# Ten dot products of the modulation weights moved from the attention stage to the context steps, and the masks loaded earlier

## The chip, the core and the metric

The kernel runs on one core of a Trainium2 chip. The metric is the device time of one execution in microseconds (us). Before the change it is 1158.29 us, the median of three runs (1157.56 to 1158.67). The engines are named as in the profile: PE is TensorE (matmul), DVE is VectorE, ACT is ScalarE, POOL is GpSimd, SP is SyncE, which here only issues DMAs.

## The reference, cut to what matters

The program is one layer of a diffusion transformer: a gated linear attention (GLA) and a short convolution side by side, an output projection, then a convolutional feed-forward net. Six vectors of 1024 numbers modulate it, and they come from one small product:

```python
def adaln(cond, w, b):
    return jax.nn.silu(cond) @ w + b          # w: 1024 x 6144

sh1, sc1, gt1, sh2, sc2, gt2 = jnp.split(adaln(c, w_ada[i], b_ada[i])[:, None, :], 6, axis=-1)
hc = modulate(rmsnorm(ctx, g_pre_mix[i]), csh1, csc1)      # context: 256 tokens
kc, vc, gfc, gbc = gla_inputs(hc @ w_in[i][:, :COL_Q], *gla_p)
hx = modulate(rmsnorm(x, g_pre_mix[i]), sh1, sc1)          # 1024 tokens
yx = token_mixers(hx @ w_in[i], s_f, s_b, ...)             # needs the gates of every token
x = x + gt1 * rmsnorm(yx @ w_out[i], g_post_mix[i])
x = x + gt2 * rmsnorm(conv_ffn(modulate(...sh2, sc2)...), g_post_ffn[i])
```

The first two vectors (`sh1`, `sc1`) are needed at the start; `gt1`, `sh2`, `sc2` and `gt2` are needed only once the attention is done.

## The kernel before

All products run on PE in three passes of float32 split into a high and a low part (`mm3`, L142; the split is ACT for the high part, then a subtraction, L135). PE's order is the program's order in the whole kernel.

**The modulation weights.** Their product is no matmul: 48 blocks of 128 rows by 1024 (512 KB each) are loaded (L223), and DVE multiplies each with the broadcast condition and sums it (`ada_dot`, L230; 16 of the blocks twice, 64 dots). `some_ada(n)` (L555) first emits the dots of the loads that are pending and then issues n more loads. A load goes into a buffer of the pool `px` (tag x, eight buffers) or into the one buffer `ada` of `pgt`, in the rotation px, pgt, px. Four of the eight hold the split context `hch` and `hcl`, and two hold `kc` and `vc`, so that in the stage of this change two and one are left: three loads can be under way, and a load waits until the dot that read its buffer before has ended.

**The token-major stage (L568 to L617).** It forms keys, values and low-rank gate inputs with tokens on the partitions: eight steps `token_major(2, tk)`, two context steps for keys (L599 to L603), two context steps `token_major(2, NT + j)`, then the same ten steps for the other half of the values, `token_major(1, ...)`. The weights of that last group are split in two parts: `wa_split(1, kt)` for kt 0 to 3 is done at the last step tk = 7, for kt 4 to 7 at L609, just ahead of `token_major(1, 0)`. ACT, DVE and POOL follow the program's order here too. `put_aT` copies the gate inputs.

**The attention stage (L734 on).** A generator `gla` and a generator `stream` (the other input projections, as half blocks of 12 matmuls) are interleaved on PE. The first two steps have DVE in the program's order; after them a scheduler orders ACT, DVE, POOL and SP by its own estimate. Each of ten 128-token tiles (two of context, then c = 0 to 7) has one gate product (L484) into one of two banks of PSUM, three passes of ACT (absolute value, exponential, logarithm), and one DVE instruction (L493) that reads the bank and writes the log decay: `gc` for context, `g` for the others. A bank is free for the gate product after the next one only when L493 has read it. `sums` (L755) are the cumulative sums, `kx_prep` and `kx_turn` (L773 to L784) the scaled keys and their transposes. Between them stood ten more dots, each with its load in the one buffer of `pgt`:

```python
                some_ada(1, (pgt, "ada", 1))        # L830 and L839
                if c == 0:
                    V.tensor_copy(masks, mraw)      # L835
```

The masks are loaded at L625, behind the last load of the token-major stage. SP issues all DMAs in one order and waits for each one's buffer there; on eight lanes a DMA also waits for the one eight places before it.

Of the kernel before, what the change touches and what calls it, by code (L numbers as in the profile page):

```python
# [8 lines left out]
F32 = mybir.dt.float32  # L9
# [12 lines left out]
P = 128  # L22
# [4 lines left out]
DK = 64  # L27
# [92 lines left out]
def build(nc, ap, out, dbg=None):  # L120
    V, S, G, PE, SY = nc.vector, nc.scalar, nc.gpsimd, nc.tensor, nc.sync
    names = iter(range(10**9))

    def nm(s="t"):
        return f"{s}{next(names)}"

    def act(o, i, fn=AF.Copy, **kw):
        return S.activation(o, i, fn, **kw)  # L128
# [13 lines left out]
    def mm3(ps, lhs, rhs, first, last, more=False):  # L142

        (lh, ll), (rh, rl) = lhs, rhs
        PE.matmul(ps, lh, rh, start=first, stop=False, skip_group_check=more)  # L145
        PE.matmul(ps, lh, rl, start=False, stop=False, skip_group_check=more)  # L146
        PE.matmul(ps, ll, rh, start=False, stop=last, skip_group_check=more)  # L147

    with tile.TileContext(nc) as tc, tc.manual_schedule(engines={mybir.EngineType.PE}):  # L149
        pools = {}  # L150

        def popen(name, side=None, **kw):
            cm = tc.tile_pool(name=name, side=side, **kw)
            pools[name] = (cm, cm.__enter__())
            return pools[name][1]
# [19 lines left out]
        def bank(n):  # L175
            return pools[n][1].tile([P, 512], F32, tag=n, name=nm("ps"))
# [30 lines left out]
        px = popen("px", "right", bufs=8)  # L207
        pgt = popen("pgt", "left", bufs=1)
# [12 lines left out]
        def ada_load(j, pool, tag, bufs):  # L221
            raw = pool.tile([P, D], F32, tag=tag, bufs=bufs, name=nm("ada"))
            SY.dma_start(raw, ap["ada"][j])  # L223
            return raw

        def ada_dot(j, which, raw, eng=None):

            dst = (gcol, gctx)[which][:, j : j + 1]
            if eng is None:
                V.tensor_tensor_reduce(raw, raw, cbs[which], 1.0, 0.0, ALU.mult, ALU.add, dst)  # L230
            else:
                eng.tensor_tensor(raw, raw, cbs[which], ALU.mult)
                act(raw, raw, AF.Copy, accum_out=dst)
# [4 lines left out]
        def ada_affine_ctx(ft):  # L238

            V.tensor_tensor(am[:, 0, ft : ft + 4, 1], gctx[:, ft : ft + 4], col("bada", ft, 4), ALU.add)  # L240
            V.tensor_tensor(am[:, 1, ft : ft + 4, 1], gctx[:, 8 + ft : 12 + ft], bsc1[:, ft : ft + 4], ALU.add)
            V.tensor_tensor(am[:, 1, ft : ft + 4, 1], am[:, 1, ft : ft + 4, 1], col("g1", ft, 4), ALU.mult)
# [47 lines left out]
        def wa_load(g, kt):  # L290
            lo = (None, 256, 528)[g]
            wars[g, kt] = pst.tile([P, 272], F32, tag="waraw", bufs=6, name=nm("war"))
            SY.dma_start(wars[g, kt], ap["wa"][kt][:, lo : lo + 272])
# [203 lines left out]
        def ctx_load():  # L497
            for j in range(NCT):
                cxs.append(x_load(ap["ctx"], j))
                cdg.append(rms_diag(cxs[j]))  # L500
# [22 lines left out]
        def hc(kt, j):  # L523
            s = slice(j * P, (j + 1) * P)
            return hch[kt // 4][:, kt % 4, s], hcl[kt // 4][:, kt % 4, s]

        def token_major(g, tk, lhs, vv):
            pp = bank(ps_mm)
            for kt in range(KT):
                mm3(pp[:, :272], lhs(kt), (wah[g, kt], wal[g, kt]), kt == 0, kt == KT - 1)  # L530
            if g == 1:
                act(vv[:, :272], pp[:, :272])
                return
            al = cp.tile([P, 32], F32, tag="al", bufs=3, name=nm("al"))
            act(al, pp[:, 240:272])
            act(vv[:, 272:], pp[:, :240])
            als[tk] = al

        def put_aT(tk):
            pt = bank(ps_ms)  # L540
            PE.transpose(pt[:32, :P], als[tk], ident)
            s = slice(tk * P, (tk + 1) * P)
            act(aT[0:32, s], pt[:32, :P])
            V.tensor_tensor(aT[32:64, s], pt[:32, :P], aT[0:32, s].bitcast(F32), ALU.subtract)
            V.tensor_copy(aT[64:96, s], pt[:32, :P])

        def xlhs(tk):
            s = slice(tk * P, (tk + 1) * P)
            return lambda kt: (hxh[kt][:, s], hxl[kt][:, s])
# [5 lines left out]
        def some_ada(n, where=None):  # L555

            for a, raw in pend:
                ada_dot(a[0], a[1], raw, a[2])
            pend.clear()
            for _ in range(n):  # L560
                a = next(adas, None)
                if a is not None:
                    where_ = where or ((px, "x", 8), (pgt, "ada", 1), (px, "x", 8))[nada[0] % 3]
                    pend.append((a, ada_load(a[0], *where_)))
                    nada[0] += 1

        als = {}
        with tc.manual_schedule(engines={mybir.EngineType.Activation, mybir.EngineType.DVE, mybir.EngineType.Pool}):  # L568
            ctx_load()
            some_ada(4)  # L570
            for hf in range(2):
                pq1 = bank(ps_mm)
                tsl = slice(hf * 512, hf * 512 + 512)
                for kt in range(KT):
                    mm3(pq1, wq1[kt], (hxh[kt][:, tsl], hxl[kt][:, tsl]), kt == 0, kt == KT - 1)
                act(qh[hf][:, 1, :], pq1, AF.Copy, scale=DK ** -0.5)
            for t in range(NT):
                vt[t] = pvo.tile([P, VW], F32, tag="vo", name=nm("v"))
            for tk in range(NT):
                some_ada(3 if tk < 3 else 2 if tk < 5 else 1)  # L580
                if tk == 3:
                    ada_affine_ctx(0)
                if tk == 5:
                    ada_affine_ctx(4)
                if 4 <= tk < 8:
                    ctx_lo()
                token_major(2, tk, xlhs(tk), vt[tk])
                if tk > 1:
                    put_aT(tk - 2)
                if 3 <= tk < 7:  # L590
                    ctx_lo = ctx_norm(tk - 3)
                if tk == NT - 1:
                    for kt in range(4):
                        wa_load(1, kt)
                        wa_split(1, kt)
            put_aT(NT - 2)
            kc = px.tile([P, NCT, QK], F32, tag="x", name="kc")
            vc = px.tile([P, NCT, VW], F32, tag="x", name="vc")
            for j in range(NCT):  # L599
                pp = bank(ps_mm)  # L600
                for kt in range(KT):
                    mm3(pp[:, :QK], hc(kt, j), (wah[0, kt][:, :QK], wal[0, kt][:, :QK]), kt == 0, kt == KT - 1)
                act(kc[:, j, :], pp[:, :QK])  # L603
            put_aT(NT - 1)
            for kt in range(4, KT):
                wa_load(1, kt)
            for j in range(NCT):
                token_major(2, NT + j, lambda kt: hc(kt, j), vc[:, j, :])
            for kt in range(4, KT):  # L609
                wa_split(1, kt)  # L610
            for tk in range(NT):
                some_ada(3 if tk < 2 else 2)
                token_major(1, tk, xlhs(tk), vt[tk])
                if 0 < tk <= NCT:
                    put_aT(NT + tk - 1)
            for j in range(NCT):
                token_major(1, NT + j, lambda kt: hc(kt, j), vc[:, j, :])  # L617
        pclose("pst")
# [2 lines left out]
        pg_ = popen("pg", "right", bufs=1)  # L621
        tc.keep_in_program_order(S.preload_act_table_set("natural_log_exp_and_others"))
        masks = pg_.tile([P, 6, DK], U8, name="masks")
        mraw = px.tile([P, 6, DK], F32, tag="x", name="mraw")
        SY.dma_start(mraw, ap["masks"])  # L625
        og_d = [dr.tile([4, P, H, P], F32, name=f"ogd{c}") for c in range(2)]
        sc_d = [dr.tile([4, P, H, P], F32, name=f"scd{c}") for c in range(2)]
        x1_d = [dr.tile([P, D], F32, name=f"x1d{c}") for c in range(NT)]
# [106 lines left out]
        def gla():  # L735
# [91 lines left out]
            slot = lambda c: su[c // 2][:, c % 2, :]  # L827
            for j in range(NCT):
                ctx_decay(j)
                some_ada(1, (pgt, "ada", 1))  # L830
                yield 1
            for c in range(NT):
                decay(c)
                if c == 0:
                    V.tensor_copy(masks, mraw)  # L835
                if 0 < c <= NCT:
                    ctx_keys(c - 1)
                if c > 1:
                    sums(c - 2)  # L839
                some_ada(1, (pgt, "ada", 1))  # L840
                if c == 4:
                    su = [px.tile([P, 2, 512], F32, tag="x", name=f"su{i}") for i in range(4)]
                    ctx_state()
                if c >= NT - 2:
                    kx_prep(0, c - NT + 2)
                yield 0.8 if c > 1 else 1
            some_ada(0)
            sums(NT - 2)
            yield 0.8
            sums(NT - 1)  # L850
# [818 lines left out]
```

## Time and profile before

| | |
|---|---|
| median of three runs | 1158.29 us |
| the profiled execution, its own time | 1158.03 us |
| its span (first to last instruction) | 1156.1 us |
| PE busy | 1120.6 us, 97% of the span |
| DVE busy | 871.7 us, 75% |
| ACT and POOL busy | 525.4 us and 493.2 us |
| mean granted clock of PE | 0.993 of full speed |
| DMA | 176.00 MB, mean 152 GB/s |
| loads of modulation weights | 64 of 512 KB, median 4.4 us from issue to landing |

An engine's busy time is the sum of its instructions. A timeline row gives the start, the time, the engine, the line and the operation, how many instructions are merged, and in brackets the idle time of the engine ahead of it with what ended it. A row of windows gives the busy time of each engine in a stretch, then the clock that PE was granted (1.00 is 2.4 GHz, 0.50 is 1.2 GHz), the share of time that the DMA engines were busy, and the rate.

### The profile page before, as it was taken

Reading aid. Unit: us, or ns where it says so; the run is one execution under the profiler, and the core shown is the slowest. Engines: PE = TensorE matmul, PEld = TensorE weight load, DVE = VectorE, ACT = ScalarE, POOL = GpSimd, SP = SyncE. Lnnn points to the kernel's source line nnn. Section 1 sums busy time; section 2 is a strip of 40 time slices with the busy share of each in tenths; the row PEclk is TensorE's granted clock in tenths of the full one; section 3 lists DMA queues with packets and bytes.
Section 4 is the critical chain, followed back from the end, with each engine's and each line's share of the span. In section 5 each row is a group of like instructions: output and inputs, shape, how many; then the busy total and the mean of one; then the engine's idle time right before and its main releaser. Section 6 shows DMA issues by size and latency. Waiting matters only on the chain. (4 is left out here: it accounts for less than half of the span.)

```text
span 1156.1 us, 16906 instructions
## 1 busy us (share of the span) xinstructions
PE 1120.6 (97%) x6272; PEld 927.1 (80%) x6272; DVE 871.7 (75%) x1195; ACT 525.4 (45%) x943; POOL 493.2 (43%) x467
## 2 busy tenths in 40 slices
PE   7899988999999999999999999999999999999997
PEld 6689977888887878887887788888888888888885
DVE  4976647899778456576888978787878787778576
ACT  5745156644343456556233343333333345544443
POOL 3211012247457111128777868687768780000002
PEclk9999999999999999999999999999999999999999
DMA  9883853421113273232343323232323169978572
GB/s 345 281 305 137 268 142 125 149 63 47 56 44 90 67 272 114 91 110 73 91 146 108 105 98 118 92 110 92 118 85 116 65 213 343 346 236 286 196 245 100
DMA packets 80132, 176.00 MB, mean 152 GB/s; under 512 B 9807, under 2 KB 21711, under 8 KB 80050
## 3 DMA queue, kind: packets, MB, share of 16 engines
q1 hardware_dynamic: 80050, 174.93, 45.6%
q8 instruction: 49, 0.80, 0.3%
q14 instruction: 33, 0.27, 0.1%
HBM read 142.12 MB, written 32.78 MB: 151 GB/s over the span
## 5 line engine op out<-in xcount | busy, mean ns | idle before, releaser
L1341 DVE SCALAR_TENSOR_TENSOR y<-u,cols,y 128x945 f32<-128x945 f32 (+2 forms) x176 | 214.6, 1221 | 3.7 <-ACT y L128 1.3
L145 PE MATMUL ps<-mx,p 128*128 128x512 f32 x440 | 173.6, 395 | 3.3 <-DVE g L1396 2.2
L146 PE MATMUL ps<-mx,p 128*128 128x512 f32 x440 | 172.9, 393 | 0.0
L147 PE MATMUL ps<-mx,p 128*128 128x512 f32 x440 | 172.7, 393 | 0.0
L135 POOL TENSOR_TENSOR p<-rs,p 128x512 fp32r<-128x512 f32 x88 | 115.3, 1315 | 86.5 <-ACT p L128 82.7
L641 POOL TENSOR_TENSOR wl<-wr,wh 128x256 fp32r<-128x256 f32 x64 | 61.2, 985 | 160.8 <-ACT wh L128 160.7
L147 PE MATMUL ps<-p,p 128*128 128x512 f32 x308 | 120.1, 390 | 0.2
L146 PE MATMUL ps<-p,p 128*128 128x512 f32 x308 | 119.9, 389 | 0.0
L145 PE MATMUL ps<-p,p 128*128 128x512 f32 x308 | 119.8, 389 | 0.0
L145 PE MATMUL ps<-hxh,wh 128*128 128x512 f32 x256 | 104.6, 408 | 1.0 <-DVE sc L699 1.0
L230 DVE CUSTOM_DVE_ANT_0 ada<-ada,cb 128x1024 f32<-128x1024 f32 x64 | 80.2, 1269 | 31.4 <-DMA ada<-in_ada 31.0
L145 PEld LDWEIGHTS ps<-mx,p 128*128 128x128 f32 x440 | 82.6, 188 | 26.2 <-ACT u L128 5.4
L147 PE MATMUL ps<-hxh,wl 128*128 128x512 f32 x256 | 100.8, 394 | 0.0
L146 PE MATMUL ps<-hxl,wh 128*128 128x512 f32 x256 | 100.6, 393 | 0.0
L128 ACT ACTIVATE p<-rs 128x512 fp32r<-128x512 f32 x88 | 54.5, 622 | 100.4 <-POOL rs L1191 100.4
L147 PEld LDWEIGHTS ps<-mx,p 128*128 128x128 f32 x440 | 82.6, 188 | 18.6
L146 PEld LDWEIGHTS ps<-mx,p 128*128 128x128 f32 x440 | 82.6, 188 | 18.3
L135 POOL TENSOR_TENSOR p<-wr,p 128x512 fp32r<-128x512 f32 x58 | 76.1, 1312 | 13.1 <-ACT p L128 13.1
L128 ACT ACTIVATE y<-u,cols 128x1024 f32<-128x1024 f32 x22 | 26.6, 1209 | 105.1 <-DVE u L1403 105.1
L145 PE MATMUL ps<-b,p 128*128 128x512 f32 x176 | 69.7, 396 | 0.0
L147 PE MATMUL ps<-b,p 128*128 128x512 f32 x176 | 69.5, 395 | 0.0
L146 PE MATMUL ps<-b,p 128*128 128x512 f32 x176 | 69.4, 395 | 0.0
(274 smaller groups left out, 2592.7 us busy)
## 6 DMA issues: line engine op xcount, KB each, us to landing
ada<-in_ada SPq DMA_DIRECT2D x64, 512.0 KB, 4.4
wr<-in_wu SPq DMA_DIRECT2D x48, 512.0 KB, 4.0
h<-hd SPq DMA_DIRECT2D x77, 256.0 KB, 4.6
hd<-h SPq DMA_DIRECT2D x73, 256.0 KB, 2.1
wdr<-in_wd SPq DMA_DIRECT2D x55, 256.0 KB, 4.1
wdr<-in_wd SPq DMA_DIRECT2D x22, 512.0 KB, 6.7
x<-in_x SPq DMA_DIRECT2D x16, 512.0 KB, 4.0
wr<-in_wb SPq DMA_DIRECT2D x16, 512.0 KB, 3.7
```

The lines of the kernel that those rows point to most:

```text
L128: return S.activation(o, i, fn, **kw)
L135: (eng or V).tensor_tensor(lo, raw, hi.bitcast(F32), ALU.subtract)
L145: PE.matmul(ps, lh, rh, start=first, stop=False, skip_group_check=more)
L146: PE.matmul(ps, lh, rl, start=False, stop=False, skip_group_check=more)
L147: PE.matmul(ps, ll, rh, start=False, stop=last, skip_group_check=more)
L230: V.tensor_tensor_reduce(raw, raw, cbs[which], 1.0, 0.0, ALU.mult, ALU.add, dst)
L641: eng.tensor_tensor(lo[:, k : k + 2], raw[:, k : k + 2], hi[:, k : k + 2].bitcast(F32), ALU.subtract)
L1341: V.scalar_tensor_tensor(y3[:, ro, co], u3[:, ri, ci], col("wcf", 9 * p + 3 * (dr_ + 1) + dc + 1), y3[:, ro, co], ALU.mult, ALU.add)
```

## The change

Two calls of `some_ada` are added at the context steps of the token-major stage (two loads each at two steps, three each at two more, ten in all), a third that only emits the last dots, ahead of the last two steps; the load of the masks moves there. The calls in `gla` go, and the cast of the masks moves from tile 0 to tile 1. Lines behind L617 move by three.

```diff
             for j in range(NCT):
                 pp = bank(ps_mm)
+                some_ada(2)
                 for kt in range(KT):
...
             for j in range(NCT):
+                some_ada(3)
                 token_major(2, NT + j, lambda kt: hc(kt, j), vc[:, j, :])
...
+            mraw = px.tile([P, 6, DK], F32, tag="x", name="mraw")
+            SY.dma_start(mraw, ap["masks"])
+            some_ada(0)
             for j in range(NCT):
                 token_major(1, NT + j, lambda kt: hc(kt, j), vc[:, j, :])
...
-        mraw = px.tile([P, 6, DK], F32, tag="x", name="mraw")
-        SY.dma_start(mraw, ap["masks"])
...
                 ctx_decay(j)
-                some_ada(1, (pgt, "ada", 1))
...
-                if c == 0:
+                if c == 1:
                     V.tensor_copy(masks, mraw)
...
-                some_ada(1, (pgt, "ada", 1))
...
-            some_ada(0)
```

DVE of the kernel before, from the last copies of the gate inputs of the token-major steps to the dots of the last group; `wal` is the low part of the weights of `token_major(1, ...)`, kt 4 to 7, and `ada` a block of modulation weights:

```order
L544 TENSOR_TENSOR aT<-ps_1258,aT 32x128
L545 CAST aT<-ps_1258 32x128
L135 TENSOR_TENSOR wal_1328<-war_1263,wah_1327 128x272
L135 TENSOR_TENSOR wal_1332<-war_1265,wah_1331 128x272
L135 TENSOR_TENSOR wal_1336<-war_1267,wah_1335 128x272
L135 TENSOR_TENSOR wal_1340<-war_1269,wah_1339 128x272
L230 ISA ada_1139,gcol<-ada_1139,cb_106 128x1024
```

The same place of DVE in the changed kernel (the numbers of the buffers differ):

```order
L230 ISA ada_1139,gcol<-ada_1139,cb_106 128x1024
...
L230 ISA ada_1208,gcol<-ada_1208,cb_106 128x1024
...
L230 ISA ada_1210,gcol<-ada_1210,cb_106 128x1024
...
L230 ISA ada_1240,gcol<-ada_1240,cb_106 128x1024
...
L230 ISA ada_1242,gcol<-ada_1242,cb_106 128x1024
...
L230 ISA ada_1284,gcol<-ada_1284,cb_106 128x1024
...
L230 ISA ada_1286,gcol<-ada_1286,cb_106 128x1024
L230 ISA gcol 128x1
L230 ISA ada_1288,gcol<-ada_1288,cb_106 128x1024
L230 ISA gcol 128x1
L135 TENSOR_TENSOR wal_1356<-war_1274,wah_1355 128x272
```

Eight dots now stand ahead of the four splits, where none stood.

DVE of the kernel before at the first gates of the attention stage; the first `gc` frees the bank of the third gate product:

```order
L230 ISA ada_1554,gcol<-ada_1554,cb_106 128x1024
L230 ISA gcol 128x1
L835 CAST masks<-mraw 128x384
L493 SCALAR_TENSOR_TENSOR gc<-ps_1727,ge_1729 128x512
L230 ISA ada_1584,gcol<-ada_1584,cb_106 128x1024
L230 ISA gcol 128x1
L230 ISA ada_1586,gcol<-ada_1586,cb_106 128x1024
L230 ISA gcol 128x1
L493 SCALAR_TENSOR_TENSOR gc<-ps_1753,ge_1755 128x512
```

The same place in the changed kernel:

```order
L230 ISA ada_1584,gcol<-ada_1584,cb_106 128x1024
L230 ISA gcol 128x1
L230 ISA ada_1614,gcol<-ada_1614,cb_106 128x1024
L230 ISA gcol 128x1
L493 SCALAR_TENSOR_TENSOR gc<-ps_1759,ge_1761 128x512
L230 ISA ada_1616,gcol<-ada_1616,cb_106 128x1024
L230 ISA gcol 128x1
L837 CAST masks<-mraw 128x384
L1032 TENSOR_TENSOR gv_4206<-gcol,cols 128x8
L1033 TENSOR_TENSOR gv_4206<-gv_4206,cols 128x8
L493 SCALAR_TENSOR_TENSOR gc<-ps_1781,ge_1783 128x512
```

The first `gc` stood behind the masks and the third last dot of the token-major stage; it now stands behind the last dot but one of all.

DVE of the kernel before between the log decays of tile 6 and tile 7 (`sc` is the short convolution, `kx` the scaled keys):

```order
L493 SCALAR_TENSOR_TENSOR g_1969<-ps_1970,ge_1972 128x512
L773 TENSOR_TENSOR kx_1989<-bc_1720 128x1024
L689 TENSOR_TENSOR sc_1820<-sc_1820,ps_1955 128x512
L773 TENSOR_TENSOR kx_2030<-bc_1721 128x1024
L230 ISA ada_1864,gcol<-ada_1864,cb_106 128x1024
L230 ISA gcol 128x1
L776 TENSOR_TENSOR kx_1989<-kx_1989,kh_92 128x1024
L693 SCALAR_TENSOR_TENSOR sc_2006<-sc_1820,cols,sc_2006 128x8x63
L493 SCALAR_TENSOR_TENSOR g_1969<-ps_2011,ge_2013 128x512
L694 SCALAR_TENSOR_TENSOR sc_2006<-sc_1820,cols,sc_2006 128x8x63
```

And in the changed kernel:

```order
L493 SCALAR_TENSOR_TENSOR g_1976<-ps_1977,ge_1979 128x512
L776 TENSOR_TENSOR kx_1993<-bc_1752 128x1024
L692 TENSOR_TENSOR sc_1839<-sc_1839,ps_1962 128x512
L776 TENSOR_TENSOR kx_2031<-bc_1753 128x1024
L779 TENSOR_TENSOR kx_1993<-kx_1993,kh_92 128x1024
L696 SCALAR_TENSOR_TENSOR sc_2010<-sc_1839,cols,sc_2010 128x8x63
L697 SCALAR_TENSOR_TENSOR sc_2010<-sc_1839,cols,sc_2010 128x8x63
L493 SCALAR_TENSOR_TENSOR g_1976<-ps_2015,ge_2017 128x512
```

The dot between them is gone, and the second half of the convolution (L694, now L697) has moved ahead of the log decay of tile 7.

## Rows read from the trace of the kernel before

**Rows 1.** The page: the busy time of each engine over the span, and the rate of the DMAs in 40 equal slices of the span.

```profile
PE 1120.6 (97%) x6272; PEld 927.1 (80%) x6272; DVE 871.7 (75%) x1195; ACT 525.4 (45%) x943; POOL 493.2 (43%) x467
...
GB/s 345 281 305 137 268 142 125 149 63 47 56 44 90 67 272 114 91 110 73 91 146 108 105 98 118 92 110 92 118 85 116 65 213 343 346 236 286 196 245 100
```

**Rows 2.** Windows of 5 us in the attention stage: the stretch, then the busy time of PE, PEld, DVE, ACT and POOL with the number of instructions, the granted clock, the DMA share and GB/s.

```profile
155.00:160.00 5.00, 2.37 (x11) 1.64 (x10) 2.90 (x5) 2.43 (x5) 0.00 (x0) 1.00 0.26 39
...
170.00:175.00 5.00, 4.33 (x16) 3.84 (x17) 3.17 (x8) 3.02 (x8) 1.54 (x2) 0.66 0.68 197
...
200.00:205.00 5.00, 5.00 (x19) 4.38 (x19) 2.97 (x4) 2.05 (x8) 0.00 (x0) 0.51 0.45 177
```

**Rows 3.** Timeline of PE in the attention stage: gate products (L484), cumulative sums (L755), and the last matmul of a half block (194.91).

```profile
155.09 0.39 PE L484 MATMUL ps<-wgh,aT 98*128 98x512 f32 x1
158.12 0.50 PE L484 MATMUL ps<-wgh,aT 98*128 98x512 f32 x1 [2.63 <-DVE gc L493]
...
167.61 1.05 PE L755 MATMUL ps<-tri,g 128*128 128x128 f32 x8
170.67 0.76 PE L484 MATMUL ps<-wgh,aT 98*128 98x512 f32 x1 [2.01 <-DVE g L493]
...
191.42 1.13 PE L755 MATMUL ps<-tri,g 128*128 128x128 f32 x8 [0.34 <-DVE g L493]
...
194.91 0.39 PE L147 MATMUL ps<-hxh,wl 128*128 128x512 f32 x1
199.35 2.05 PE L755 MATMUL ps<-tri,g 128*128 128x128 f32 x8 [4.05 <-DVE g L493]
```

**Rows 4.** Timeline of DVE in the attention stage, with the idle time ahead of an instruction in brackets.

```profile
157.10 0.36 DVE L835 CAST masks<-mraw 128x384 uint8<-128x384 f32 x1 [3.18 <-DMA mraw<-in_masks]
157.38 0.68 DVE L493 SCALAR_TENSOR_TENSOR gc<-ps,ge 128x512 f32<-128x512 f32 x1
...
168.55 1.45 DVE L230 CUSTOM_DVE_ANT_0 ada<-ada,cb 128x1024 f32<-128x1024 f32 x1 [6.31 <-DMA ada<-in_ada]
...
169.94 0.68 DVE L493 SCALAR_TENSOR_TENSOR g<-ps,ge 128x512 f32<-128x512 f32 x1
...
183.75 1.22 DVE L230 CUSTOM_DVE_ANT_0 ada<-ada,cb 128x1024 f32<-128x1024 f32 x1 [2.38 <-DMA ada<-in_ada]
...
184.90 0.68 DVE L689 TENSOR_TENSOR sc<-sc,ps 128x512 f32<-128x512 f32 x1
...
194.05 1.76 DVE L230 CUSTOM_DVE_ANT_0 ada<-ada,cb 128x1024 f32<-128x1024 f32 x1
...
195.74 1.73 DVE L776 TENSOR_TENSOR kx<-kx,kh 128x1024 f32<-128x1024 f32 x1
...
198.52 0.68 DVE L493 SCALAR_TENSOR_TENSOR g<-ps,ge 128x512 f32<-128x512 f32 x1
199.12 0.73 DVE L694 SCALAR_TENSOR_TENSOR sc<-sc,cols,sc 128x504 f32<-128x504 f32 x1
199.78 1.21 DVE L776 TENSOR_TENSOR kx<-kx,kh 128x1024 f32<-128x1024 f32 x1
```

**Rows 5.** Timeline of ACT: the scaling of the short convolution that holds up ACT's queue ahead of the log decays of tiles 5 to 7.

```profile
185.62 0.82 ACT L128 ACTIVATE sc<-sc,cols 128x512 f32<-128x512 f32 x1 [1.92 <-DVE sc L689]
```

**Rows 6.** Timeline of SP in the token-major stage: the DMAs that it issued, merged (a row spans from the first issue to the last).

```profile
108.69 0.80 SPq L293 DMA_DIRECT2D war<-in_wa  x2
115.49 3.12 SPq L634 DMA_DIRECT2D wr<-in_wb  x2
118.70 33.01 SPq L223 DMA_DIRECT2D ada<-in_ada  x18
```

**Rows 7.** The tile of the modulation weights over the whole kernel: its dots on DVE (ns shortest, median, longest) and the time of its loads from issue to landing.

```profile
L230 DVE CUSTOM_DVE_ANT_0 ada<-ada,cb x64: 1208/1224/2323, 13.9 to 218.9; 128x1024 f32<-128x1024 f32 x64
...
DMA to landing us min/median/max: 3.5/4.4/9.0
```

**Rows 8.** Timeline of DVE in the token-major stage: the copies of the gate inputs (L545), the splits of the weights of kt 4 to 7 (L135), and dots.

```profile
110.04 0.28 DVE L545 CAST aT<-ps 32x128 fp32r<-32x128 f32 x1
...
113.80 0.28 DVE L545 CAST aT<-ps 32x128 fp32r<-32x128 f32 x1
119.90 1.50 DVE L135 TENSOR_TENSOR wal<-war,wah 128x272 fp32r<-128x272 f32 x4 [5.81 <-ACT wah L128]
121.31 1.22 DVE L230 CUSTOM_DVE_ANT_0 ada<-ada,cb 128x1024 f32<-128x1024 f32 x1
...
123.36 1.23 DVE L230 CUSTOM_DVE_ANT_0 ada<-ada,cb 128x1024 f32<-128x1024 f32 x1 [0.82 <-DMA ada<-in_ada]
...
131.35 1.22 DVE L230 CUSTOM_DVE_ANT_0 ada<-ada,cb 128x1024 f32<-128x1024 f32 x1
...
132.50 1.22 DVE L230 CUSTOM_DVE_ANT_0 ada<-ada,cb 128x1024 f32<-128x1024 f32 x1
...
152.69 1.22 DVE L230 CUSTOM_DVE_ANT_0 ada<-ada,cb 128x1024 f32<-128x1024 f32 x1 [1.33 <-DMA ada<-in_ada]
```

**Rows 9.** Windows of the dots alone: the stretch, DVE's busy time with the number of dots, the granted clock, the DMA share and GB/s.

```profile
140.00:155.00 15.00, 8.38 (x7) 1.00 0.85 279
```

**Rows 10.** Timeline of PE at the first step of the last group of the token-major stage: its first matmul, and the first that reads a low part of kt 4.

```profile
118.89 0.29 PE L145 MATMUL ps<-wah,hxh 128*128 128x272 f32 x1
...
120.52 0.29 PE L146 MATMUL ps<-wal,hxh 128*128 128x272 f32 x1
```

## The prediction, made before the changed kernel ran

> **What bounds the kernel now.** I read the page first: PE is busy for 1120.6 of 1156.1 us [rows 1], so only PE's own waits and PE's slow clock can be won. Listing PE's waits by stage, I find 9 of the 35 us of idle time in one stretch, 155 to 205 us, the start of the attention stage: 2.63 us ahead of the third gate product (158.12), 2.01 ahead of the sixth (170.67), 0.34 and 4.05 ahead of the last cumulative sums (191.42, 199.35), each ended by a log decay on DVE [rows 3]. The windows add that PE was granted 0.66 of full speed in 170 to 175 and 0.51 in 200 to 205, each time behind such a wait [rows 2]; that is 0.34 x 4.33 = 1.5 us and 0.49 x 5 = 2.45 us lost.
>
> DVE's timeline tells why the decays are late. The first stood behind the cast of the masks, which waited 3.18 us for its DMA; the one at 169.94 behind a dot that waited 6.31 us for its weights; between the decays of tiles 6 and 7 DVE did a dot from 194.05 to 195.74 [rows 4]. The change removes the masks from that place, and all ten dots. The question is what the ten cost where they go.
>
> **The token-major stage: DMAs.** Here DVE and the DMAs have room before, and PE runs without a gap. But the loads are a closed loop: three buffers, a median of 4.4 us from issue to landing, then a dot of 1.22 us [rows 7] that steps on by 1.15 (131.35 to 132.50), and only then the next issue. The 16 dots from 123.36 to 152.69 [rows 8] give 29.33 / 15 = 1.955 us each; (4.4 + 1.15) / 3 = 1.85 would be the loop with nothing else in it. So ten more loads cost about 19.6 us of loop time. Before, SP issued only small loads and two blocks of other weights between 108.69 and 118.70, and then 18 loads in 33.01 us [rows 6]; the new loads can fill those 10 us and not the rest.
>
> I step through it. The dot of the load that was already there follows the copies of the gate inputs (110.04 + 0.28, rows 8): 110.34. Behind it stand two dots whose buffers come free early, and SP has nothing else to issue until 108.69 [rows 6], so their loads have landed: 111.5 and 112.65, to 113.8, then a copy to 114.4. The dot at 110.34 frees a buffer at 111.6; its load lands 4.0 later (I take 3.5 to 4.4, few loads being under way), so the next dots stand at 115.6 and 116.75, then 117.9 (loaded 112.8 to 117). The buffer freed at 116.8 lands at 120.9: dots at 120.95 and 122.1, to 123.25.
>
> **A new wait at 120.5.** Only behind these eight dots come the four splits of kt 4 to 7. Before, they ran at 119.90 [rows 8], and PE read the first low part at 120.52 [rows 10], with no slack to speak of. Now the first split ends at 123.25 + 0.4 = 123.7: PE waits 3.2 us (2.5 to 4.5 by the same landing times). Nothing but the rest of this product is queued behind it on PE; ACT's evictions follow PE.
>
> **A longer wait at the third gate.** Behind the splits (1.5 us) the loop goes on: the dot after them at 124.7, the next, loaded at 122.2, at about 126.6. From that dot to the last but one, behind which the first log decay now stands, are 18 steps: 126.6 + 18 x 1.955 = 161.8, the decay at 163.0. PE follows a decay by 158.12 - 157.38 = 0.74 [rows 3, 4]: the third gate product comes at 163.7 in place of 158.12. That is 5.6 us late, and it swallows the wait at 120.5, since PE would arrive at 155.48 + 3.2 = 158.7. The step is 1.85 at the low end (1.9 us earlier) and 2.14 at the high end, as in 140 to 155, where seven dots took 15 us [rows 9] (3.3 us later); I take 1.955, the mean of the same loop.
>
> PE then sits idle for 5 us. The nearest wait, 4.05 us, was followed by 0.51 [rows 2], the shorter 2.63 by full speed. I count one such stretch, 2.45 us, less the 0.34 us or so that PE waits for the next gate's bank anyway: 2.1 us. Its ends are 0 and 2.45.
>
> A rule of the Trainium skill would give another end: DMA: Bandwidth & Descriptors, section Bandwidth, puts the limit of HBM to SBUF near 358 GB/s per core; as an estimate from it, 512 KB would take 1.46 us, and a loop bound by that would be faster than I have it. The trace does not agree in this stage, with 279 GB/s at a DMA share of 0.85 [rows 9]; by that rule the 18 steps end 9 us earlier.
>
> **What goes away in the attention stage.** Removed there: ten loads and ten dots of 1.2 us, which lay beside PE's work except where a decay stood behind them.
> - The decay at 169.94 had its bank's data long before; without the dot ahead of it, it runs by 165 and PE comes to 170.67 without the 2.01 us; the slow clock behind it (1.5 us) goes too. Both ends: 0 if that clock stays, 3.5; I take 3.5, since DVE has nothing else to do there.
> - The 0.34 us at 191.42: I take it as gone.
> - Tile 7. ACT's queue waited 1.92 us at 185.62 for the convolution on DVE [rows 5], which stood behind a dot that waited for its load (183.75, then 184.90); DVE had idled 2.38 us ahead of that dot, and would have taken the convolution then. So ACT is some 2 us earlier from there, and with it the decay of tile 6. Between the two decays DVE saves the dot (195.74 - 194.05 = 1.7) and gains the half convolution that is now ahead (199.78 - 199.12 = 0.66) [rows 4]. The decay of tile 7: 198.52 - 2 - 1.7 + 0.66 = 195.5, and 0.7 more for it. PE arrives at 194.91 + 0.39 = 195.3 [rows 3], and waits 0.9 in place of 4.05: 3.1 us. With so short a wait the slow clock of 200 to 205 goes too, 2.45. The ends are 0, if ACT's queue holds as before, and 6.5 with no wait left.
>
> The masks' cast costs 0.36 us behind the last dot; nothing at that place reads them. The two blocks of stream weights that SP issued from 115.49 on now stand behind loads; they are read only in the attention stage, past 155. The small write of the second row of gains moves ahead of two such blocks, for which nothing waits yet: 0, and at the other end a landing, 4.4 us, if one of them were late. From 205 us on PE works at 97% and more, so what is won or lost by then reaches the end.
>
> **The sum**, against the profiled execution's own 1158.03 us (span 1156.1 and 1.9 around it, 0.26 below the median of the runs): + 5.6 (third gate) + 2.1 (clock behind it) - 3.5 (170.67) - 0.3 - 3.1 - 2.5 (tile 7, wait and clock) = 1156.3 us.
>
> **The rivals.**
> 1. *The loads run at the rate of the DMA engines.* The first slice of the page moves 345 GB/s [rows 1]; 0.524 MB at that rate is 1.52 us, and 18 steps end at 126.6 + 27.4 = 154.0, before PE arrives at 158.7. Only the wait at 120.5 is left (158.7 in place of 158.12): + 0.6 in place of + 7.7, so 1149.2. For it: the added loads come at a quiet place. Against it: the loop of before never went so fast, with the same three buffers. 10%. The limit that the Trainium skill gives (DMA: Bandwidth & Descriptors, section Bandwidth) would fall on this side.
> 2. *Slower: ACT's order keeps tile 7 where it is.* ACT works through its queue in order, and its exponential of the scaled keys waits for DVE, the scaling for the convolution, and only then comes tile 7's absolute value. If that chain starts with PE's gate rather than with the dots, the 4.05 us and the slow clock behind them stay, 5.6 us, while the late third gate is paid: 1161.9. It decides from the point where tile 7's decay comes more than some 2.5 us behind PE's 195.3 on the old scale. For it: the decay of tile 6 waited for ACT, not for a dot. Against it: rows 5 show ACT itself waiting for DVE. A loop step of 2.14 adds 3.3 us and brings the same sign: 1159.6. 23% together.
> 3. *No change:* the late gate and the freed stage cancel to within 1 us, since PE only waits at another place: 1158. For it: both sums are near 8 and 9 us. 17%.
> 4. *My forecast*, 1156.3, 50%, with an own range of 1153.5 to 1159 from the ends of the loop step and the clock.
>
> **How the numbers follow.** A change of less than 0.2% (2.3 us) can't be told from none here; against the median that is 1156.0 to 1160.6. My forecast lies at this edge: 24 of its 50% below, 26 inside. Faster: 24 + 10 + 6 of rival 3 = 40%. Slower: 21 of rival 2's 23. Same: 26, 11 of rival 3 and 2 of rival 2, 39%. The range leaves out most of rival 1 and the top of rival 2: 1151.5 to 1161.8.
>
> **What would show it.** In the profile of the changed kernel: a wait of PE of about 3 us near 120.5 for a split (L135); a wait of about 5 us ahead of the third gate product for the first decay, DVE's dots going on to about 163 us in steps of 1.95, with waits for DMAs between; a slow clock behind it; no wait ahead of the sixth gate; under 1.5 us ahead of the last sums, at full clock. I would be wrong if the third gate comes within 2 us of its old time, or if tile 7's wait keeps its 4 us.

## The result, and the profile after

The changed kernel takes 1161.88 us (median of 22 runs, 1158.58 to 1166.58) against 1159.24 of the kernel before on the same chip (22 runs, 1157.27 to 1163.24): ratio 1.002, 95% interval 1.0011 to 1.0029. It is slower by 0.2%, where I had forecast 0.2% faster. The profiled execution has a span of 1159.4 us, 3.3 more than before.

PE's busy time on the page hardly moves [rows 1]; its waits do:

```profile
PE 1121.8 (97%) x6272; PEld 929.1 (80%) x6272; DVE 873.6 (75%) x1195; ACT 524.8 (45%) x943; POOL 495.3 (43%) x467
```

The timeline of PE has the new wait for the split (124.36; 120.52 before [rows 10]), the third gate product (165.83), the sixth (178.41, without a wait) and the last two cumulative sums [rows 3]:

```profile
124.36 0.59 PE L146 MATMUL ps<-wal,hxh 128*128 128x272 f32 x1 [4.15 <-DVE wal L135]
...
165.83 0.80 PE L484 MATMUL ps<-wgh,aT 98*128 98x512 f32 x1 [4.96 <-DVE gc L493]
...
178.41 0.48 PE L484 MATMUL ps<-wgh,aT 98*128 98x512 f32 x1
...
196.67 1.95 PE L758 MATMUL ps<-tri,g 128*128 128x128 f32 x16
203.41 1.13 PE L758 MATMUL ps<-tri,g 128*128 128x128 f32 x8 [2.04 <-DVE g L493]
```

The windows [rows 2] show where the clock fell (the number ahead of the DMA share) behind the two long waits, and that it holds now from 200 on:

```profile
120.00:125.00 5.00, 0.85 (x4) 0.65 (x4) 4.97 (x12) 0.71 (x3) 1.63 (x2) 0.92 0.72 251
125.00:130.00 5.00, 5.00 (x32) 5.00 (x32) 2.73 (x6) 0.40 (x1) 0.00 (x0) 0.74 0.94 342
165.00:170.00 5.00, 4.17 (x10) 3.32 (x11) 3.49 (x10) 2.86 (x5) 0.00 (x0) 0.52 0.21 4
170.00:175.00 5.00, 5.00 (x20) 4.06 (x19) 1.00 (x3) 2.49 (x5) 0.00 (x0) 0.80 0.00 0
200.00:205.00 5.00, 2.96 (x19) 2.40 (x19) 4.37 (x6) 3.23 (x8) 3.25 (x3) 1.00 0.17 29
205.00:210.00 5.00, 5.00 (x29) 4.27 (x29) 4.54 (x5) 4.18 (x10) 0.00 (x0) 1.00 0.82 281
```

DVE's timeline [rows 4, 8] tells why: the splits stand behind eight dots, then come the dots of the loop, from 126.84 on, and behind the last but one (163.93) the first log decay. At the end the decay of tile 7 (202.59) runs behind a half convolution:

```profile
115.18 1.82 DVE L230 CUSTOM_DVE_ANT_0 ada<-ada,cb 128x1024 f32<-128x1024 f32 x1 [1.33 <-DMA ada<-in_ada]
...
120.30 0.68 DVE L1032 TENSOR_TENSOR gv<-gcol,cols 128x8 f32<-128x8 f32 x1
...
122.72 1.21 DVE L230 CUSTOM_DVE_ANT_0 ada<-ada,cb 128x1024 f32<-128x1024 f32 x1
...
123.87 1.49 DVE L135 TENSOR_TENSOR wal<-war,wah 128x272 fp32r<-128x272 f32 x4
...
126.84 1.23 DVE L230 CUSTOM_DVE_ANT_0 ada<-ada,cb 128x1024 f32<-128x1024 f32 x1 [0.34 <-DMA ada<-in_ada]
...
130.08 1.23 DVE L230 CUSTOM_DVE_ANT_0 ada<-ada,cb 128x1024 f32<-128x1024 f32 x1 [2.01 <-DMA ada<-in_ada]
...
132.61 1.23 DVE L230 CUSTOM_DVE_ANT_0 ada<-ada,cb 128x1024 f32<-128x1024 f32 x1 [1.29 <-DMA ada<-in_ada]
...
163.93 1.23 DVE L230 CUSTOM_DVE_ANT_0 ada<-ada,cb 128x1024 f32<-128x1024 f32 x1 [1.26 <-DMA ada<-in_ada]
...
165.08 0.69 DVE L493 SCALAR_TENSOR_TENSOR gc<-ps,ge 128x512 f32<-128x512 f32 x1
...
200.32 1.22 DVE L696 SCALAR_TENSOR_TENSOR sc<-sc,cols,sc 128x504 f32<-128x504 f32 x1
201.57 1.10 DVE L697 SCALAR_TENSOR_TENSOR sc<-sc,cols,sc 128x504 f32<-128x504 f32 x1
202.59 0.68 DVE L493 SCALAR_TENSOR_TENSOR g<-ps,ge 128x512 f32<-128x512 f32 x1
```

The 18 steps of the loop from 126.84 to 163.93 took 2.06 us each, but not evenly: the first two (126.84 to 132.61) took 5.77 us together, the other 16 took 1.96 each. SP's timeline shows what was new at the start of the loop. The second block of stream weights (`wr`, 512 KB like a load) was issued ahead of the loads before [rows 6]; it now comes at 124.41, between them:

```profile
120.40 3.90 SPq L223 DMA_DIRECT2D ada<-in_ada  x3
124.41 0.37 SPq L637 DMA_DIRECT2D wr<-in_wb  x1
126.53 34.43 SPq L223 DMA_DIRECT2D ada<-in_ada  x18
```

The three loads issued around it, from 123.9 to 128.5, took 5.9 us to land (median), the block 6.8:

```profile
ada<-in_ada SPq DMA_DIRECT2D x3, 512.0 KB, 5.9
wr<-in_wb SPq DMA_DIRECT2D x1, 512.0 KB, 6.8
```

The loads' tile over the whole kernel, and with it the time from issue to landing, 4.7 in place of 4.4 [rows 7]:

```profile
L230 DVE CUSTOM_DVE_ANT_0 ada<-ada,cb x64: 1209/1224/2320, 13.2 to 165.7; 128x1024 f32<-128x1024 f32 x64
...
DMA to landing us min/median/max: 3.4/4.7/9.1
```

Put side by side at the same instructions, after stands 5.4 us behind before at the first gate product (157.50 against 152.12), 7.7 at the third, 10.0 at the fifth (176.07 against 166.08), 7.7 at the sixth, 6.7 at the seventh (182.97 against 176.26), 4.1 at the last sums, and 1.5 at the second transpose of the scaled keys (207.59 against 206.11). These figures count from the start of the execution. At the first matmul of the last group (118.25; 118.89 before [rows 10]), ahead of every wait that the change makes, the changed kernel stood 0.6 us ahead by earlier waits that the change does not touch, so counted from there it lost 2.1 us by the second transpose. The other 1.8 of the 3.3 us come far from the change: 0.5 lost at 412.84, 0.3 won back near 523, and 1.6 lost behind a wait at 539 that both kernels have (last section).

### The profile page after: what moved, and what is told of

The parts are those of the page before. It is cut to its first block, busy times and chain, and to the rows that moved or that the text cites. A ratio compares the mean times of both kernels' runs of the same rounds, so it can differ in the third digit from the quotient of the medians.

```text
span 1159.4 us, 16904 instructions
## 1 busy us (share of the span) xinstructions
PE 1121.8 (97%) x6272; PEld 929.1 (80%) x6272; DVE 873.6 (75%) x1195; ACT 524.8 (45%) x943; POOL 495.3 (43%) x467
## 5 line engine op out<-in xcount | busy, mean ns | idle before, releaser
L135 POOL TENSOR_TENSOR p<-rs,p 128x512 fp32r<-128x512 f32 x88 | 115.3, 1315 | 88.1 <-ACT p L128 84.3
L135 POOL TENSOR_TENSOR p<-wr,p 128x512 fp32r<-128x512 f32 x58 | 76.2, 1313 | 13.1 <-ACT p L128 13.1
```

What stands on the lines that cost most here:

```text
L135: (eng or V).tensor_tensor(lo, raw, hi.bitcast(F32), ALU.subtract)
```

## The experiments

Loop theory means here: the third gate product waits until the closed loop of loads and dots is through, and the waits ahead of it on PE cost nothing. All ratios are to the kernel before, from runs on the same chip; all differences are small, and I call one faster or slower where its 95% interval leaves out 1. Where an edit adds lines, the lines behind it move: the gate product is L484 or L485.

**The masks alone.** The hunks of the masks, without the dots:

```diff
-        mraw = px.tile([P, 6, DK], F32, tag="x", name="mraw")
-        SY.dma_start(mraw, ap["masks"])
...
+            mraw = px.tile([P, 6, DK], F32, tag="x", name="mraw")
+            SY.dma_start(mraw, ap["masks"])
...
-                if c == 0:
+                if c == 1:
                     V.tensor_copy(masks, mraw)
```

> The kernel before with the masks alone moved (their load behind the token-major tiles, their cast behind the second tile's decay); all ten dots stay in the attention stage. Loop theory (each wait is set by what stands ahead of the decay on DVE): the 2.63 us ahead of the third gate product go, it comes at about 155.5; the wait ahead of the sixth stays or grows, since its dot waits for a load; 1.5 to 2.6 us faster than before, near 1157. Rival (the wait only goes on to the next gate): no change, 1159.

1158.31 us against 1157.90, ratio 1.0001 (0.9989 to 1.0013): the rival's number, but not its reason, since the edit did not take the masks away from the first decay. The load, in a buffer that a dot must free, was issued at 155.74, the scheduler put the cast ahead of the first decay all the same, and PE still waited 2.7 us at the third gate product. DVE's timeline:

```profile
158.57 0.36 DVE L835 CAST masks<-mraw 128x384 uint8<-128x384 f32 x1 [2.86 <-DMA mraw<-in_masks]
158.84 0.68 DVE L493 SCALAR_TENSOR_TENSOR gc<-ps,ge 128x512 f32<-128x512 f32 x1
```

**What the ten dots cost at all.**

```diff
             for j in range(NCT):
                 pp = bank(ps_mm)
-                some_ada(2)
...
             for j in range(NCT):
-                some_ada(3)
                 token_major(2, NT + j, lambda kt: hc(kt, j), vc[:, j, :])
```

> The changed kernel without the ten loads and dots at the context steps; they are left out altogether (gcol is cleared once instead, so ten of its columns stay zero). It prices the ten dots wherever they stand. Loop theory: no wait at the split, third gate product near 155.5, the sixth gate's wait gone, tile 7's at most 2 us at full clock: 1146 to 1150. Rival (the waits of the attention stage are ACT's and stay): 1155 to 1158.

1154.42 us, ratio 0.9966 (0.9953 to 0.9980): faster, but by a third of what I expected. The attention stage gave what theory says, from 3.7 us late at the fourth gate product (165.36 against 161.68) to 4.7 early at the second transpose of keys (201.44), 8.4 us; but PE still waits 5.5 us ahead of the third gate product, because the loop's last dot stands at 155.78 and the masks' cast behind it waits for a load issued only at 153.55:

```profile
160.06 0.80 PE L485 MATMUL ps<-wgh,aT 98*128 98x512 f32 x1 [5.47 <-DVE gc L494]
```

**Is the wait at the split worth its 4 us?**

```diff
+            for kt in range(4, KT):
+                wa_split(1, kt)
             for j in range(NCT):
                 some_ada(3)
                 token_major(2, NT + j, lambda kt: hc(kt, j), vc[:, j, :])
-            for kt in range(4, KT):
-                wa_split(1, kt)
```

> The changed kernel with the four splits of kt 4 to 7 ahead of the dots that stood in front of them. Loop theory: no wait of PE near 120, PE arrives at the third gate product at about 155.5, and this still comes at 165.8 to 168, when the loop of the loads is through; PE waits about 10 us there in one piece; the time is that of the changed kernel, or up to 2.5 us more, 1162 to 1164. Rival (what was lost is the wait of 4.15 us at the split and the clock behind it): 5 to 6 us less, 1156.

1166.47 us, ratio 1.0072 (1.0060 to 1.0084). PE does not wait near 120 and saves nothing; it waits 15.9 us at the third gate product. That is 4.4 us later than in the changed kernel, more than I expected, for two reasons. The splits waited on DVE for their high parts (2.4 us ahead of 115.72), and the dots with them. And the write of a row of gains, issued at 122.94, came into the loop: the two loads behind it took 10.1 and 10.2 us to land, and DVE waited for them (its timeline, then PE's):

```profile
132.26 1.23 DVE L230 CUSTOM_DVE_ANT_0 ada<-ada,cb 128x1024 f32<-128x1024 f32 x1 [5.16 <-DMA ada<-in_ada]
```

```profile
170.20 0.79 PE L484 MATMUL ps<-wgh,aT 98*128 98x512 f32 x1 [15.91 <-DVE gc L493]
```

**Is the loop's step set by buffers or by the DMA engines?** A fourth buffer; `wgl` moves to make room:

```diff
-        wgh, wgl = (pgt.tile([NG, 2 * QK], F32R, name=n) for n in ("wgh", "wgl"))
+        wgh = pgt.tile([NG, 2 * QK], F32R, name="wgh")
+        wgl = pst.tile([NG, 2 * QK], F32R, tag="t", bufs=4, name="wgl")
-                    where_ = where or ((px, "x", 8), (pgt, "ada", 1), (px, "x", 8))[nada[0] % 3]
+                    where_ = where or ((px, "x", 8), (pgt, "ada", 1), (px, "x", 8), (pst, "ad2", 1))[nada[0] % 4]
```

> The changed kernel with a fourth buffer in the rotation of the weight loads (4 KB a partition from the pool of the token-major stage). Loop theory (landing time over number of buffers): the step of the loop falls from 2.06 to 1.4 to 1.6 us, the last dot but one ends by about 156, PE no longer waits at the third gate product and loses no clock there: 5 to 8 us less than the changed kernel, 1154 to 1157. Rival (the step is what the DMA engines give): step 1.85 to 2.06, third gate product at 162 to 166, 0 to 4 us less, 1158 to 1162.

1153.44 us, ratio 0.9965 (0.9954 to 0.9977), faster than both kernels. Over the same 18 dots the step is (155.26 - 126.01) / 18 = 1.63 us in place of 2.06. Not all of that is the buffer: here SP issued both blocks of stream weights only behind the loop (153.36 and 153.83). Against the 1.96 us of the changed kernel behind its block, the step is 0.33 smaller; 18 of these are 6 of the 8.7 us by which the last dot but one comes earlier, some 1.9 are the block, and 0.8 the earlier start:

```profile
126.01 1.21 DVE L230 CUSTOM_DVE_ANT_0 ada<-ada,cb 128x1024 f32<-128x1024 f32 x1
...
155.26 1.23 DVE L230 CUSTOM_DVE_ANT_0 ada<-ada,cb 128x1024 f32<-128x1024 f32 x1
```

The window of the dots alone has ten in place of eight, at 331 GB/s in place of 236 (the changed kernel first, then this one; 279 before [rows 9]):

```profile
140.00:155.00 15.00, 9.23 (x8) 1.00 0.76 236
```

```profile
140.00:155.00 15.00, 11.68 (x10) 1.00 0.91 331
```

PE's timeline keeps the wait at the split and loses the one at the gate:

```profile
123.94 0.60 PE L146 MATMUL ps<-wal,hxh 128*128 128x272 f32 x1 [3.96 <-DVE wal L135]
...
161.04 0.50 PE L485 MATMUL ps<-wgh,aT 98*128 98x512 f32 x1 [0.54 <-DVE gc L494]
```

**Would fewer dots do?** Five moved (1 and 1 at the context keys, 1 and 2 at the values), five left; three buffers, then four:

```diff
-                some_ada(2)
+                some_ada(1)
...
-                some_ada(3)
+                some_ada(1 + j)
...
+                if c < 6:
+                    some_ada(1 if c < 5 else 0, (pgt, "ada", 1))
```

> The changed kernel with five of the ten dots moved (1, 1, 1 and 2 at the context steps) and the other five in the attention stage, behind the decays of tiles 0 to 4, none between the decays of tiles 6 and 7; three buffers as before. Loop theory (the quiet place takes in some four loads, each further one costs a step of 2.06 us at the third gate): the splits stand behind four dots and PE waits under 1 us near 120; the loop ends some 10 us earlier than in the changed kernel, third gate product at 156 to 158; tile 7's wait near 2 us; 1152 to 1156. Rival (dots left in the attention stage hold up decays there as before): 1157 to 1160.

> The same with the fourth buffer as well. Loop theory: the loop is through by 150, no wait of PE near 120 and none ahead of the third gate product (155 to 156), full clock from there on: 1147 to 1151. Rival (the waits only move on to the next gates of the attention stage): 1153 to 1156.

Both missed: 1167.23 us (ratio 1.0085, 1.0071 to 1.0098) and 1160.81 (1.0026, 1.0016 to 1.0036). I had left SP's queue out of account. With three buffers the next loads stood behind two blocks of stream weights, the second of which waited 3.9 us for POOL; from 111.1 to 119.85 no load was issued, so the quiet place took in nothing. PE waited 9.7 us at the third gate product, and 4.1 more at the fourth, since the first dot left had waited 7.2 us for a load issued behind the write of a row of gains. SP's timeline:

```profile
108.77 2.36 SPq L223 DMA_DIRECT2D ada<-in_ada  x2
115.67 4.09 SPq L637 DMA_DIRECT2D wr<-in_wb  x2
119.85 1.33 SPq L223 DMA_DIRECT2D ada<-in_ada  x3
```

With four, the loop was through at 152.2, but the scheduler put the first of the dots left ahead of the first decay, and its load was issued at 150.73, just behind the write of a row of gains (149.97). DVE's timeline:

```profile
162.49 1.23 DVE L230 CUSTOM_DVE_ANT_0 ada<-ada,cb 128x1024 f32<-128x1024 f32 x1 [9.68 <-DMA ada<-in_ada]
163.64 0.69 DVE L494 SCALAR_TENSOR_TENSOR gc<-ps,ge 128x512 f32<-128x512 f32 x1
```

**Four buffers, and the wait at the split taken away.** First by shifting two loads to later tiles, then by putting the splits between dots, then like the second with eight dots moved (`some_ada(2)` there) and two left at tiles 2 and 3:

```diff
-                some_ada(3)
+                some_ada((1, 3)[j])
...
-                some_ada(3 if tk < 2 else 2)
+                some_ada(3 if tk < 4 else 2)
```

```diff
             for j in range(NCT):
+                if j == 1:
+                    for kt in range(4, KT):
+                        wa_split(1, kt)
                 some_ada(3)
```

> The changed kernel with four buffers, and with two of the loads of the context steps shifted to the third and fourth token-major tile, so that five dots in place of eight stand ahead of the four splits. Loop theory: the wait of 4 us at the split falls to 0 to 1.5 us, but the loop still ends at about 157 and the third gate product stays near 159 to 161, so 0 to 2 us come of it: 1151.5 to 1153.5. Rival (the wait at the split is worth its full 4 us and its clock): 1148 to 1150.

> The changed kernel with four buffers and, on DVE, the four splits of kt 4 to 7 behind five dots in place of eight; the loads stay in their order. Loop theory: the wait near 120 falls to 0.3 to 1.2 us, but the loop ends no earlier than with four buffers alone (its last dots at 157 to 160), and ACT's first gate tile, whose place the fourth buffer holds until its last dot, follows that; third gate product at 161 to 164, so no faster than four buffers alone: 1153 to 1157. Rival (the 4 us at the split count in full): 1149 to 1150.

> The same with eight of the ten dots at the context steps and two in the attention stage (loads at the tiles 2 and 3). Loop theory: two steps of 1.63 less, the loop ends 3.3 us earlier than with ten, third gate product at 157.5 to 160; the first of the two left stands ahead of the second decay and holds it only if its load lands after 161: 1149 to 1152. Rival (what is left in the attention stage holds a decay up again, as with five moved): 1154 to 1158.

1157.46 (ratio 0.9995, 0.9984 to 1.0005), 1158.18 (1.0010, 0.9995 to 1.0024) and 1157.37 us (1.0006, 0.9992 to 1.0019): each gives away what four buffers had won. In the first two the wait near 120 shrinks to 1.1 and 0.25 us, and PE waits 7.1 and 7.4 us at the gate. One cause is the fourth buffer itself: ACT's first gate tile takes its place in memory and waits for the last dot (ACT's timeline of the first):

```profile
160.67 0.60 ACT L128 ACTIVATE ge<-ps 128x512 f32<-128x512 f32 x1 [7.89 <-DVE gcol L230]
```

In the third a dot that was left held the second decay for 5.8 us, waiting for a load that was issued at 157.03 with a row write right behind it.

**The end of the fourth buffer freed.**

```diff
-                    where_ = where or ((px, "x", 8), (pgt, "ada", 1), (px, "x", 8), (pst, "ad2", 1))[nada[0] % 4]
+                    where_ = where or ((px, "x", 8), (pgt, "ada", 1), (px, "x", 8), (pst, "ad2", 1) if nada[0] < 47 else (px, "x", 8))[nada[0] % 4]
```

> The kernel with four buffers, the last load of the rotation put in another buffer than the fourth, so that the gate tile that takes the fourth buffer's place is free four dots earlier. Splits as in the changed kernel (behind eight dots). Theory (with four buffers the third gate product waited only 0.5 us, since PE came 4 us late from the split): 0 to 0.5 us less than with four buffers, 1153 (ratio 0.996 to 0.997). Rival (the gate tile's place sets the time): 2 us less, 1151.

> The same with the four splits behind five dots in place of eight. Here the gate tile's place did hold the first decay (2.1 us of idle time of DVE behind the last dot and before the decay, for ACT). Theory: PE does not wait at the split, the decay follows the last dot but one, third gate product at 158.5 to 161 in place of 163.7; 1 to 4 us less than with the splits between and the place not freed, 1152 to 1155. Rival (PE's long wait and the clock behind it decide, whatever ended it): 1156 to 1158.

1154.08 us (ratio 0.9968, 0.9956 to 0.9981) and 1153.45 (0.9960, 0.9946 to 0.9974), both as the theory had it. With the splits between, the gate product stands at 158.66 behind 3.3 us of waiting and nothing was lost at 120; by the second transpose of keys that is no better than four buffers alone (200.31 against 199.96), since a wait of 3 to 4 us is paid once in either.

**POOL beside DVE.**

```diff
-            w = block(2)
+            w = stream_weights(ap["wb"][2], V)
```

> The changed kernel with the low parts of the first streamed block subtracted on DVE, not on POOL, so that POOL is idle from 112 to 122. Theory (DVE's dots last 1.75 to 1.82 us there, and not 1.22, because POOL works at the same time): all dots from 115 to 121 last 1.22 us. Rival (they are slow because of the DMAs that write at 272 GB/s): they stay at 1.75. The low parts put four more instructions ahead of the splits on DVE, so the wait near 120 may stay; the loop and the third gate product by at most 1.5 us either way.

1168.89 us (2 runs), ratio 1.0100 (1.0080 to 1.0121). The dots at 118.50 and 119.64 lasted 1.22 us and the small addition behind them 0.16, where the changed kernel has 1.75 and 0.68, and DMAs moved 227 GB/s in 119 to 121; the one at 116.82, beside the end of POOL's work on the next block, still took 1.75. The DMAs were busier in the changed kernel (385 GB/s in 119 to 121), so this run alone does not part POOL from them; but the changed kernel's dot at 126.84 took 1.23 us in a window of 342 GB/s without POOL, which speaks against the rival. The total says nothing on POOL, since the write of a row came into the loop, and cost it a wait of 7.8 us:

```profile
118.50 1.22 DVE L230 CUSTOM_DVE_ANT_0 ada<-ada,cb 128x1024 f32<-128x1024 f32 x1
...
120.79 0.16 DVE L1032 TENSOR_TENSOR gv<-gcol,cols 128x8 f32<-128x8 f32 x1
...
138.11 1.22 DVE L230 CUSTOM_DVE_ANT_0 ada<-ada,cb 128x1024 f32<-128x1024 f32 x1 [7.77 <-DMA ada<-in_ada]
```

## Why the prediction was wrong

- **The third gate, + 5.6.** The failed step: it cost 7.7 us. The mechanism was right, a closed loop that the third gate waits for; what it left out was the second block of stream weights, for which I had put 0 because nothing waits for it yet. The dot at which I started the loop came at 126.84 (126.6 forecast), and 18 steps took 37.09 us, 2.06 each and not 1.955; that is 1.9 of the 2.1 us. The excess lies in the first two steps, 5.77 us in place of 3.91, where the block landed between the loads; the 16 steps behind them took 1.96, as forecast. (Cut one dot later, at 133.88, the first three steps hold 1.2 of the 1.9.) Loops with three buffers and no block in them agree with the 1.955: 1.90 in the five-moved run ((160.73 - 124.56) / 19) and 1.96 in the run without the ten dots ((155.78 - 122.41) / 17). No run moved the block alone, so that it cost the 1.9 us is argued from these rows. I had this case as the high end of a range and as part of the slower rival (2.14, 1159.6 us), and put too little chance on it.
- **The wait at 120.5, 3.2 us, swallowed.** It was 4.15 us, since PE came there 0.6 us earlier than before and three dots and two additions ahead of the splits lasted longer beside POOL (115.18 and 120.30, last section), with a slow clock behind it that I had not priced (0.74 in 125 to 130). Both were swallowed all the same: PE came to the gate at 160.87 and waited 4.96 more. In the run with the splits ahead that wait is gone, and PE waits the longer at the gate. With four buffers, too, the runs with and without it stand equal at the second transpose.
- **The clock behind the gate, + 2.1.** From the third gate product to the fifth, 2.3 more us were lost, at 0.52.
- **The sixth gate, - 3.5.** Right: from the fifth to the seventh 3.3 us came back, the wait and the clock.
- **Tile 7 and the 0.34 us, - 5.9 together.** 5.2 us from the seventh gate product to the second transpose. The wait is 2.04, not 0.9: ACT was done with tile 7 at 201.32, but DVE stood in a half convolution, whose two instructions took 1.22 and 1.10 us (0.73 for the one in rows 4) beside POOL's work. It stayed 2.0 in every variant that emptied the end of the stage. The clock of 200 to 205 held, as forecast.
- **The masks, 0.** The cast stood behind the last dot (166.83) and cost nothing there, as forecast. What moving the masks is worth by itself stays open: alone, the edit left the cast ahead of the first decay.
- **The row of gains, 0 at this place.** True here, because both writes fell behind the last load. My other end, a landing of 4.4, was too short: the two writes took 13.9 at the longest.
- **The rival of the DMA rate.** The order of 345 GB/s was there to be had: 331 with a fourth buffer. With three it was out of reach, as I argued. The figure near 358 GB/s that I took from the Trainium skill (DMA: Bandwidth & Descriptors, section Bandwidth), which that section gives for a core whose neighbour on the same memory streams as well, bound nothing here; in 113 to 115 the changed kernel moved 389.

Up to the second transpose I forecast - 1.7 us and 1.5 came, counted from the start of the execution: 2.1 from the third gate, 0.2 from its clock, 0.2 from the sixth, 0.7 from tile 7. That is the sign. The medians are 2.6 us apart and the two profiles 3.3; what lies behind the second transpose is mostly the clock of one wait (last section).

## What to carry to other kernels

Work moved to a stage with idle engines is not free there if it comes through a closed loop: its price is at least (landing time + use) / buffers per item. Here that is (4.4 + 1.15) / 3 = 1.85 us, and 1.90 to 1.96 were measured. Before moving the work one should ask for one more buffer: here it was worth 0.33 us per load, and together with the block out of the loop it turned the sign of the change. What else is issued into the loop counts too, even if nothing waits for it: a block of 512 KB at its start went with 1.9 us lost. A wait of PE that stands ahead of a later, fixed event is no target; take away the event first. And of each moved load, look at what stands ahead of it in the issuing queue: here two waiting blocks and a 4 KB write cost more than any dot.

## What the runs showed of the hardware

- **A 4 KB write that starves the loads.** The row of gains is written out as a column, 1024 elements of four bytes (1174 packets under 512 B in 124 to 146 of the run with the low parts on DVE). It took 13.9 us to land in the changed kernel, 12.7 in that run, where all DMAs together then moved 64 GB/s, at a DMA share of 1.43 (the number ahead of the rate), and the loads beside it took 11.4 to 12.8 us to land; in two other runs loads issued just behind such a write took 10.1 to 11.6:

```profile
127.00:130.00 3.00, 3.00 (x21) 3.00 (x20) 1.62 (x3) 0.40 (x1) 0.00 (x0) 0.75 1.07 347
130.00:133.00 3.00, 3.00 (x26) 2.97 (x25) 0.34 (x2) 0.55 (x2) 0.00 (x0) 1.00 1.43 64
```

  The Trainium skill (DMA: Bandwidth & Descriptors, section Specifications) asks for at least 512 B in a transfer for full rate; the trace agrees, and shows that the other loads pay as well.
- **DVE beside POOL.** Dots of 1.22 us took 1.73 to 1.82 while POOL subtracted low parts, and two additions of 8 columns 0.68 and 0.65 in place of 0.16 and 0.17. Not every one: with four buffers a dot at 118.45 took 1.21 inside POOL's stretch. The Trainium skill (SBUF — State Buffer, section SBUF: two separate sides) has the two engines lock each other out of a shared port; the rows fit that in the main, and in the run without POOL's work there the two dots are short. The short dot inside POOL's stretch stays unexplained.
- **The same wait, two clocks.** Behind a wait of PE of 2.16 us at 537.66 before and of 2.17 at 539.36 after, the clock was 1.00 in the one execution and 0.86 in the other, before first:

```profile
532.00:544.00 12.00, 9.84 (x43) 7.75 (x42) 7.30 (x9) 4.86 (x8) 11.92 (x9) 1.00 0.29 89
```

```profile
532.00:544.00 12.00, 9.83 (x37) 7.63 (x36) 8.06 (x9) 5.70 (x9) 11.18 (x8) 0.86 0.29 89
```

  PE fell 1.6 us behind there, against 1.5 us from the change in these two profiles. The same wait stands in all fourteen profiles of this case, 1.78 to 2.17 us long: in five the clock held behind it (waits of 1.78, 1.78, 1.81, 2.00 and 2.16), in nine it fell (1.82 to 2.17), for some 1.6 us each time. So the clock behind a wait of some 2 us should be forecast as a chance, not as a yes or no.
